# One level of Strassen's algorithm in the input projection of a hybrid attention layer, its weights prepared on the chip

## The chip, the cores and the metric

The kernel runs on one core of a Trainium2 chip. The metric is the device time of one execution in microseconds. Three runs of the kernel before took 1495.16, 1495.91 and 1497.05 us; the median is 1495.91 us. A second, profiled execution gives the trace that the text reads.

Five engines run their own instruction streams: PE (TensorE: matmuls and transposes), DVE (VectorE), ACT (ScalarE), POOL (GpSimd) and SP (SyncE), which in this kernel issues every DMA. Each works through its stream in the order in which the program wrote it, and waits on semaphores of the others. Matmul results land in PSUM banks, all other tiles in SBUF.

## What is computed

One layer on a sequence of 1024 tokens of width 1024, in float32. The input projection has 3080 columns: queries, keys and values of eight forgetting heads, eight gate columns, and queries, keys and values of eight chunked heads.

```python
h = rmsnorm(x, g_mix_pre[l])
proj = h @ w_in[l]                      # 1024 x 1024 by 1024 x 3080
y_fox = forgetting_attention(fq, fk, fv, f_logit)
y_chk = chunked_relpos_attention(cq, ck, cv, rel_bias[l])
y = concat(rmsnorm(y_fox), rmsnorm(y_chk))
x = x + rmsnorm(y @ w_out[l], g_mix_post[l])
x = x + rmsnorm(memory_cross_attention(rmsnorm(x, g_mem_pre[l]), mem_n, ...), g_mem_post[l])
x = x + rmsnorm(square(relu(rmsnorm(x, g_ff_pre[l]) @ w_ff1[l])) @ w_ff2[l], g_ff_post[l])
```

A forgetting head attends to all earlier tokens, with a bias from the cumulated log of its gate; a chunked head attends to its own chunk of 64 and the eight before it, with a bias by relative position.

## The kernel before

**Precision.** Every float32 operand of a product is split into a high part (rounded to the matmul's format) and a low part (the rest), and each product is three matmuls: high by high, high by low, low by high (`mm3`, L191 to L195). A split is a copy on ACT and a difference on DVE or POOL.

**Prologue** (L1346 to L1398, an order written out by hand). Rows of x are loaded, normalised (`norm_x`), turned by PE into the layout with features on partitions and split (`to_T`, L208 to L232). While this goes on, the values of four forgetting and four chunked heads are computed (`values`, in two groups of 256 columns; group 0 also has the eight gate columns) from weights that `value_weights` loads and `value_split` splits.

**Attention phase** (`attention_phase`). A planner (`Flow`) writes the order of all engines. It keeps a time for each engine, takes the next step of PE from the first of several streams that is ready, and places the work of the other engines with costs given in the code. The streams, by rank: products of probabilities and values (`value_steps`), transposes of probabilities (`turn_steps`), scores (`score_steps`), small jobs (`side_steps`), and as filler the rest of the projection (`filler_steps`: `project_steps` for query, key and late values of each pair of heads, 16 matmul groups for each block of 128 columns), then the memory's keys and values (`memory_steps`). `Stock` loads weights in order (tag `wraw`, three buffers) and splits them into the tags `whi` and `wlo` (two buffers each) or into the pool `u4`. Chunked heads 0 to 3 come first, then the forgetting heads, then the other chunked heads (`ORDER`). Scores are padded to at least 256 columns (`wide = max(w, 256)`, L581). Where a query block doesn't see a key block, `turn_steps` has POOL write zeros into that quarter (L665, L666), and `value_steps` multiplies all four quarters (L708, L709). Each block of outputs is summed from two halves by ACT (L715) and DVE (L716) and stored to DRAM (`od`). `forget_gates` computes the gates' bias from the projection's eight columns, in two exponentials and a logarithm on ACT and passes on DVE.

**After it.** `second_filler` begins with the output projection of the forgetting heads (`mix_steps(0)`), then of the chunked heads (`mix_steps(1)`), then memory attention and the MLP, which is already a Strassen product of one level. The MLP is not touched.

Of the kernel before, what the change touches and what calls it, by code (L numbers as in the profile page):

```python
# [14 lines left out]
F32 = mybir.dt.float32  # L15
# [7 lines left out]
P = 128  # L23
# [112 lines left out]
def build(ctx, tc, nc, out, t):  # L136
# [16 lines left out]
    def u4(name, shape, dt=F32R):  # L153

        return up.tile(list(shape), dt, tag="u4", bufs=30, name=name)
# [16 lines left out]
    wcount = [0]  # L172

    def load_w(src, shape, alloc=None, lo_on=None):
        n = wcount[0]
        wcount[0] += 1
        raw = wp.tile(shape, F32, tag="wraw", bufs=3, name=f"wraw{n}")
        nc.sync.dma_start(raw, src)
        return split_w(raw, shape, n, alloc, lo_on)

    def split_w(raw, shape, n, alloc=None, lo_on=None):
        if alloc is None:
            hi = wp.tile(shape, F32R, tag="whi", bufs=2, name=f"whi{n}")
            lo = wp.tile(shape, F32R, tag="wlo", bufs=2, name=f"wlo{n}")
        else:
            hi, lo = alloc(f"whi{n}", shape), alloc(f"wlo{n}", shape)
        nc.scalar.activation(hi, raw, AF.Copy)
        (lo_on or nc.gpsimd).tensor_sub(lo, raw, f(hi))
        return hi, lo

# [15 lines left out]
    def rms(x, scratch, name):  # L206
        ss = small.tile([P, 1], F32, tag="ss", bufs=8, name=f"ss_{name}")
        nc.scalar.activation(scratch, x, AF.Square, scale=1.0 / 32.0, accum_out=ss)  # L208
        return rstd_of(ss, f"rstd_{name}")

    def to_T(xa, xb, act, c0, name, tags=("tr", "tr")):

        trs = [mm_tile([P, 2, 2, P], f"tr_{name}_{k}", tags[k // 4]) for k in range(0, KC, 2)]

        def turn(k, q):
            xn = (xa, xb)[q]
            for j in range(2):
                nc.tensor.transpose(trs[k // 2][:, j, q, :], xn[:, (k + j) * P:(k + j + 1) * P], ident)

        ahead = tags[0] != tags[1]  # L220
        if ahead:
            for k in range(0, KC, 2):
                turn(k, 0)
        for k in range(0, KC, 2):
            if not ahead:
                turn(k, 0)
            turn(k, 1)
            src = trs[k // 2].rearrange("p a q b -> p a (q b)")
            i, o = k // act.per, k % act.per
            dh = act.h[i][:, o:o + 2, c0:c0 + 256]  # L230
            nc.scalar.activation(dh, src, AF.Copy)
            nc.vector.tensor_sub(act.l[i][:, o:o + 2, c0:c0 + 256], src, f(dh))  # L232


# [6 lines left out]
    ones = const.tile([1, P], F32, name="ones")  # L241
    nc.vector.memset(ones, 1.0)
# [3 lines left out]
    od = [[dr.tile([P, HT], F32, name=f"od{k}_{h}") for h in range(2)] for k in range(KC)]  # L246
# [3 lines left out]
    md = [dr.tile([P, D], F32, name=f"md{b}") for b in range(2)]  # L250
# [3 lines left out]
    p1s = ExitStack()  # L254
    p1 = pool("p1", stack=p1s)
# [6 lines left out]
    hT = [Act(f"hT{h}") for h in range(2)]  # L262
    def load_x(b):
        tag = "sp" if b % 3 else "klo"
        xt = p1.tile([P, D], F32, tag=tag, bufs=5 if b % 3 else 4, name=f"x_{b}")
        nc.sync.dma_start(xt, t["x"][b * P:(b + 1) * P, :])
        return xt

    def norm_x(xt, b):
        junk = p1.tile([P, D], BF16, tag="ph", bufs=2, name=f"junk{b}")  # L270
        r = rms(xt, junk, f"x{b}")
        nc.vector.scalar_tensor_tensor(xt, xt, r, gpre, op0=ALU.mult, op1=ALU.mult)
# [3 lines left out]
    def bias_rows(part):  # L276

        if part == 0:
            rows.extend(p1.tile([8, 768], F32, tag="sp", bufs=5, name=k) for k in ("rrow", "rsrc"))
# [8 lines left out]
    fcol = p1.tile([P, TB, 8], F32, tag="o2", bufs=2, name="fcol")  # L288

    def value_weights(g, raws=None, only=None):  # L290

        n = 264 if g == 0 else 256
        src = t["w_v0"] if g == 0 else t["w_v1"]
        raws = [] if raws is None else raws
        for i, (a, b) in enumerate(((0, 3), (3, 6), (6, 8)) if g == 0 else ((0, 4), (4, 8))):
            if only in (None, i):
                raw = wp.tile([P, b - a, n], F32, tag="wraw", bufs=3, name=f"wrawv{g}{a}")
                nc.sync.dma_start(raw, src[:, a:b, :])
                raws.append(raw)
        return raws  # L300

    def value_split(g, raw, i, lo_on=None):
        k = raw.shape[1]
        wh, wl = split_w(raw, list(raw.shape), f"v{g}{i}", None if g == 1 else u4, lo_on)
        return [(wh[:, j, :], wl[:, j, :]) for j in range(k)]

    def value_tiles(g):

        return [u4(f"vs{g}_{i}", (P, 2, 4, P)) for i in range(4)]

    def values(g, w, vs, kb):
        act, cs = hT[kb // 4], slice((kb % 4) * P, (kb % 4 + 1) * P)
        n = 264 if g == 0 else 256
        ps = mm_tile([P, n], f"v{g}_{kb}")
        for kc in range(KC):
            mm3(ps, act.hi(kc, cs), act.lo(kc, cs), *w[kc], kc == 0, kc == KC - 1)
        src = ps[:, 0:256].rearrange("p (h d) -> p h d", d=64)
        dh = vs[kb // 2][:, kb % 2, :, 0:64]
        nc.scalar.activation(dh, src, AF.Copy)
        if g == 0:  # L320
            nc.scalar.activation(fcol[:, kb, :], ps[:, 256:264], AF.Copy)
        nc.vector.tensor_sub(vs[kb // 2][:, kb % 2, :, 64:128], src, f(dh))


    ORDER = (("c", 0), ("c", 1), ("f", 0), ("f", 1), ("f", 2), ("f", 3), ("c", 2), ("c", 3))
# [3 lines left out]
            dict(s=2, tr=2, pv=2, mm=2, sp=1, p=2, klo=4, bias=2, raw=2, w=0, u4=6,  # L329
# [16 lines left out]
    class Stock:  # L346
# [3 lines left out]
        def __init__(self):  # L350
            self.blocks = []
            for n, (kind, pr) in enumerate(ORDER):
                if n == 5:
                    self.blocks.append("norm")
                b = (0 if kind == "f" else 8) + pr
                self.blocks.append((("q", n), t["w_qk"][b], [P, KC, P]))
                if n > 3:
                    self.blocks.append((("v", n), t["w_v"][n - 4], [P, KC, P]))
                if n == 7:
                    self.blocks.append("mem")  # L360
                self.blocks.append((("k", n), t["w_qk"][b + 4], [P, KC, P]))
# [53 lines left out]
        def split_now(self, n):  # L415
            for _ in range(n):
                key = self.to_split.pop(0)
                self.hi(key)
                for half in range(2):
                    self.lo(key, nc.gpsimd, half)  # L420
# [1642 lines left out]
```

## Time and profile before

| what | value |
|---|---|
| median of three runs | 1495.91 us |
| span of the profiled execution, first to last instruction | 1496.5 us |
| PE waits longest for another engine | 2.6 us in four places, products of probabilities and values |
| DMA traffic of the execution | 218.58 MB, 146 GB/s on average |
| DMA in the first 60 us | 8.00 MB |

The profile gives no other time of its own execution than the span; the span is 0.6 us above the median of the runs. In the rows, "L193" is line 193 of the kernel, "out<-in" names the tiles, and a row of the timeline gives start and duration in us, the engine, the line, the operation and, in brackets, how long the engine had been idle before it and what ended that. "PEld" is the loading of a matmul's stationary operand, which overlaps PE. A matmul's duration is the time until its end in the pipeline; what one costs in a row of them is the distance between their starts.

### The profile page before, as it was taken

Reading aid. Unit: us, or ns where it says so; the run is one execution under the profiler, and the core shown is the slowest. Engines: PE = TensorE matmul, PEld = TensorE weight load, DVE = VectorE, ACT = ScalarE, POOL = GpSimd, SP = SyncE. Lnnn points to the kernel's source line nnn. Section 1 sums busy time; section 2 is a strip of 40 time slices with the busy share of each in tenths; the row PEclk is TensorE's granted clock in tenths of the full one; section 3 lists DMA queues with packets and bytes.
Section 4 is the critical chain, followed back from the end, with each engine's and each line's share of the span. In section 5 each row is a group of like instructions: output and inputs, shape, how many; then the busy total and the mean of one; then the engine's idle time right before and its main releaser. Section 6 shows DMA issues by size and latency. Waiting matters only on the chain. (4 is left out here: it accounts for less than half of the span.)

```text
span 1496.5 us, 21618 instructions
## 1 busy us (share of the span) xinstructions
PE 1475.1 (99%) x7628; PEld 1254.1 (84%) x7628; DVE 938.1 (63%) x1617; ACT 789.8 (53%) x1405; POOL 403.4 (27%) x629
## 2 busy tenths in 40 slices
PE   8999999999999999999999999999999999999998
PEld 7989888888889888888888887888888888888886
DVE  6377677565576834884375577775555675646577
ACT  5367576575666835554354455555555553444442
POOL 4244355353354300521031423333333000000021
PEclk9999999999999999999999999999999999999999
DMA  4223312512225552461241355774445685436465
GB/s 170 90 74 89 84 44 88 152 55 65 73 66 149 173 177 85 137 213 59 85 169 57 112 183 186 265 246 147 150 150 176 234 340 202 140 120 215 173 252 197
DMA packets 82766, 218.58 MB, mean 146 GB/s; under 512 B 9801, under 2 KB 13905, under 8 KB 82658
## 3 DMA queue, kind: packets, MB, share of 16 engines
q1 hardware_dynamic: 82658, 217.20, 43.5%
q8 instruction: 60, 0.98, 0.3%
q14 instruction: 48, 0.39, 0.1%
HBM read 157.86 MB, written 50.91 MB: 140 GB/s over the span
## 5 line engine op out<-in xcount | busy, mean ns | idle before, releaser
L677 DVE TENSOR_TENSOR pl<-ptr,ph 128x512 fp32r<-128x512 f32 (+1 forms) x152 | 92.2, 616 | 39.7 <-ACT ph L680 33.7
L1789 ACT ACTIVATE whif<-ra 128x1024 fp32r<-128x1024 f32 x37 | 39.2, 1060 | 122.2 <-PE fy L194 62.6
L1791 DVE TENSOR_TENSOR wlof<-ra,whif 128x1024 fp32r<-128x1024 f32 x37 | 45.3, 1225 | 91.0 <-ACT whif L1789 91.0
L680 ACT ACTIVATE ph<-ptr 128x512 fp32r<-128x512 f32 (+1 forms) x152 | 79.3, 540 | 39.0 <-PE ptr L671 32.4
L1905 POOL TENSOR_SCALAR rf<-sf 128x1 f32<-128x1 f32 x8 | 8.2, 1026 | 326.4 <-ACT jf L1890 326.1
L709 PE MATMUL pv<-pl,vs 128*128 128x256 f32 x304 | 78.9, 283 | 2.6 <-DVE pl L677 2.6
L708 PE MATMUL pv<-ph,vs 128*128 128x256 f32 x304 | 79.8, 286 | 0.0
L194 PE MATMUL fx<-vlof,whif 128*128 128x512 f32 x168 | 65.4, 389 | 0.0
L193 PE MATMUL fx<-vhif,whif 128*128 128x512 f32 x168 | 65.4, 389 | 0.0
L195 PE MATMUL fx<-vhif,wlof 128*128 128x512 f32 x168 | 65.4, 389 | 0.0
L709 PEld LDWEIGHTS pv<-pl,vs 128*128 128x128 f32 x304 | 57.6, 189 | 7.4 <-DVE pl L677 2.2
L708 PEld LDWEIGHTS pv<-ph,vs 128*128 128x128 f32 x304 | 57.3, 188 | 4.0
L1679 POOL TENSOR_TENSOR sc<-wf,wf 128x512 f32<-128x512 f32 x14 | 21.3, 1524 | 142.3 <-DMA wf<-in_w_ff 95.4
L193 PE MATMUL k<-hT_hi,whik 128*128 128x512 f32 x128 | 52.7, 412 | 0.0
L193 PE MATMUL mq<-h2T_hi,whimq 128*128 128x512 f32 x128 | 51.6, 403 | 0.0
L193 PE MATMUL q<-hT_hi,whiq 128*128 128x512 f32 x128 | 50.9, 398 | 0.0
L193 PE MATMUL ym<-whimo,oT_hi 128*128 128x512 f32 x128 | 50.3, 394 | 0.1
L194 PE MATMUL yw<-wlowo,yT_hi 128*128 128x512 f32 x128 | 49.9, 390 | 0.3 <-DVE wlowo L410 0.3
L195 PE MATMUL k<-hT_hi,wlok 128*128 128x512 f32 x128 | 50.2, 392 | 0.0
L194 PE MATMUL mq<-h2T_lo,whimq 128*128 128x512 f32 x128 | 50.1, 391 | 0.1
L193 PE MATMUL yw<-whiwo,yT_hi 128*128 128x512 f32 x128 | 50.1, 392 | 0.0
L194 PE MATMUL k<-hT_lo,whik 128*128 128x512 f32 x128 | 50.1, 391 | 0.0
(596 smaller groups left out, 5029.2 us busy)
## 6 DMA issues: line engine op xcount, KB each, us to landing
ra<-gd SPq DMA_DIRECT2D x56, 512.0 KB, 3.9
wg<-in_w_ff SPq DMA_DIRECT2D x56, 512.0 KB, 6.0
wf<-in_w_ff SPq DMA_DIRECT2D x38, 512.0 KB, 4.0
gd<-s SPq DMA_DIRECT2D x48, 256.0 KB, 2.1
wrawmq<-in_w_mq SPq DMA_DIRECT2D x16, 512.0 KB, 3.8
wrawmo<-in_w_mo SPq DMA_DIRECT2D x16, 512.0 KB, 3.8
gd<-u SPq DMA_DIRECT2D x32, 256.0 KB, 2.1
gd<-g SPq DMA_DIRECT2D x25, 256.0 KB, 2.5
```

The costliest lines, as they stand in the source:

```text
L193: nc.tensor.matmul(ps, lh, rh, start=start, stop=False, skip_group_check=more)
L194: nc.tensor.matmul(ps, lh, rl, start=False, stop=False, skip_group_check=more)
L195: nc.tensor.matmul(ps, ll, rh, start=False, stop=stop, skip_group_check=more)
L677: flow.put("V", at, 0.7, lambda: nc.vector.tensor_sub(pl[:, live, :], tr[:, live, :], f(ph[:, live, :])), done)
L680: flow.put("S", flow.end, 0.6, lambda ph=ph, tr=tr, live=live: nc.scalar.activation(ph[:, live, :], tr[:, live, :], AF.Copy), split)
L708: nc.tensor.matmul(pv, v, ph[:, hs, :], start=c == 0 and half == 0, stop=False)
L709: nc.tensor.matmul(pv, v, pl[:, hs, :], start=False, stop=c + 1 == len(steps) and half == 1)
L1679: eng.tensor_sub(sc[:, k1], r0[:, k0], r1[:, k0])
L1789: nc.scalar.activation(ah, ra, AF.Copy)
L1791: nc.vector.tensor_sub(al, ra, f(ah))
L1905: nc.gpsimd.tensor_scalar(r, ssf[b][:, 0:1], ssf[b][:, 1:2], EPS, op0=ALU.add, op1=ALU.add)
```

## The change

With x split into quadrants by feature half and token half, and each pair of weight blocks (query and key columns of two heads, or 512 columns of forgetting values and 512 of chunked values) split into quadrants by feature half and column kind, one level of Strassen's algorithm (in Winograd's form) makes seven products of what were eight. Four sums of the weights and four sums of x's quadrants are formed first, and seven sums of the results afterwards.

- **x** comes a second time, transposed by the host (`x_t`). The rows are loaded only for their squares; the inverse norms are written to DRAM (`rsd`) and read back spread over all partitions (`rstd4`), and multiply the transposed tiles (`norm`). The first two value products use x times its gain alone and scale their rows afterwards.
- **Prologue.** Two value products; the first query product of all eight pairs from the two quadrants of the first 512 tokens (`q_prod`, with weights loaded and split in the loop), their finals, and a stored first product (`pqd`); meanwhile sums of x; memory rows are normalised and turned here; gate products (`gate_prod`); then the other five value products with their sums, with the gate chain cut into four pieces between them (`gate_chain`).
- **Attention phase.** Each pair has five products left (`pair_steps`); POOL forms the weight sums and copies the high parts (`pair_sums`, `pair_splits`), DVE the low parts. Queries, keys and values all go to DRAM (`qkd`, `vsd`) and are fetched for each head (`Heads`). Forgetting heads come first. After the pairs the filler is: memory keys, the output projection of the forgetting heads (results stored in `yd`, read back by `Back`), memory values.
- **Probabilities by values.** No zeros are written: a matmul covers only the quarters that hold something, so it may be 128 columns wide. Outputs are copied by one ACT instruction and stored as two halves (`od` doubles); the halves are added when they are read back.
- **Planner.** `u4` has 33 buffers in place of 30; some costs and token counts differ; all splits of later weights have their low part on DVE.

```diff
-        return up.tile(list(shape), dt, tag="u4", bufs=30, name=name)
+        return up.tile(list(shape), dt, tag="u4", bufs=33, name=name)
...
+    def rstd4(ss, th):
+        r = rall[:, th * 4:th * 4 + 4]
+        nc.gpsimd.tensor_scalar(r, ss, EPS, None, op0=ALU.add)
+        nc.gpsimd.tensor_tensor(r, r, mhalf[:, 0:4], op=ALU.pow)
+        nc.sync.dma_start(rsd[th * 4:th * 4 + 4, :].rearrange("b p -> p b"), r)
+        rt = pro.tile([P, HT], F32, tag="rt", bufs=2, name=f"rt{th}")
+        row = rsd[th * 4:th * 4 + 1, :]
+        nc.sync.dma_start(rt, bass.AP(tensor=row.tensor, offset=row.offset, ap=[[0, P], [1, HT]]))
+        return rt
...
-    ORDER = (("c", 0), ("c", 1), ("f", 0), ("f", 1), ("f", 2), ("f", 3), ("c", 2), ("c", 3))
+    ORDER = tuple((kind, pr) for kind in "fc" for pr in range(4))
...
-                for half in range(2):
+                full = 1 if dead == [0] else 0
+                todo = [(full, ph), (1 - full, ph), (1 - full, pl), (full, pl)]
+                for m, (half, x) in enumerate(todo):
...
+                    qs_ = [k for k in (2 * half, 2 * half + 1) if k not in dead]
+                    k0, k1 = qs_[0], qs_[-1] + 1
+                    q0 = slots[k0][1]
+                    nc.tensor.matmul(pv[:, q0:q0 + k1 - k0, :], v, x[:, k0:k1, :], start=c == 0 and m == 0,
+                                     stop=c + 1 == len(steps) and m == 3, skip_group_check=True)
...
+        yield from prod("6", 0, 0, quads["T2"], ([("pair", n, 0), ("p1", n)], True, 2))
...
+        yield from prod("5", 1, 0, quads["T1"], ([("pair", n, 1)], True, 2))
...
+        yield from prod("7", 2, 0, quads["T3"], ([("pair", n, 2), key("u2")], False, 2))
...
+        yield from prod("3", 0, 4, quads["B22"], ([key("p5")], False, 0))
...
+        yield from prod("4", 1, 4, quads["T4"], ([key("u3")], False, 0))
...
+        for _ in zip(load_xt(0, 0, True), load_v(0, 0, True)):
+            pass
+        list(load_xt(0, 1))
+        list(load_v(0, 1))
+        xrow = [load_row(b) for b in range(4)]
...
+        def vsplit(raw, name, eng, cut=False):
+            w = [wp.tile([P, 2, HT], F32R, tag=x, bufs=2, name=f"{x}v{name}") for x in ("whi", "wlo")]
+            for c in (slice(0, 1), slice(1, 2)) if cut else (slice(0, 2),):
+                yield nc.scalar.activation(w[0][:, c, :], raw[:, c, :], AF.Copy)
+                eng.tensor_sub(w[1][:, c, :], raw[:, c, :], f(w[0][:, c, :]))
+            yield w
...
+        for kp in range(4):
+            list(load_xt(1, kp))
+        xrow += [load_row(b) for b in range(4, 8)]
...
+        def values_out(k, kb, src):
+            st = u4(f"vst{k}{kb}", (P, 8, P))
+            v = src.rearrange("p (h d) -> p h d", d=64)
+            nc.scalar.activation(st[:, :, 0:64], v, AF.Copy)
+            nc.vector.tensor_sub(st[:, :, 64:128], v, f(st[:, :, 0:64]))
+            nc.sync.dma_start(vsd[k][:, :, kb, :], f(st).rearrange("p (n x) c -> p n (x c)", x=2))
...
+        def split_q(n):
...
+            nc.scalar.activation(w[0], raw, AF.Copy)
+            nc.gpsimd.tensor_sub(w[1], raw, f(w[0]))
...
+        for s in range(9):
+            if s < 8:
+                qb[s] = mm_tile([P, HT], f"q{s}", ("mm", "s")[s % 2])
+                q_prod(s, 0, B11)
+            if s:
+                q_prod(s - 1, 1, B21)
...
+            if s < 8:
+                q_first(s)
+            if s + 3 < 8:
+                load_q(s + 3)
+                split_q(s + 3)
+            if s:
+                q_final(s - 1)
+            for call in items[:3 if s < 2 else 2]:
+                call()
...
+        vprod(X, quads["T2"], w, True)
+        w = vw(4, "s3")
+        gate_chain(4)
...
+        for b in range(4):
+            nc.vector.tensor_add(u2[b], X[b], p1v[b])
+        vprod(X, quads["T3"], w, False)
+        w = vw(3, "a22")
+        gate_chain(4)
...
+        for b in range(4):
+            g = g_pro(f"u3v{b}")
+            nc.vector.tensor_add(f(g), X[b], p1v[b])
+            nc.vector.tensor_add(f(g), Z[b], f(g))
+            values_out(1, 4 + b, f(g))
+        vprod(X, quads["T4"], w, False)
```

More of the change, by code (lines that the diff above doesn't have):

```diff
@@ new lines, in build, with __init__, pump, load @@
+    p1r = {}
+    class Firsts:
+        def __init__(self):
+            self.left = list(range(8))
+        def pump(self):
+            while self.left and free["g"].ready():
+                n = self.left[0]
+                if n and not there(("u3", n - 1)):
+                    break
+                self.left.pop(0)
+                free["g"].take()
+                def load(n=n):
+                    p1r[n] = g_tile(f"p1r{n}")
+                    nc.sync.dma_start(f(p1r[n]), pqd[n])
+                flow.load(flow.now, load, mark(("p1", n)), 3.0)
```

978 lines of the change are left out of this document (596 added, 382 removed).

## The prediction

> **What bounds the kernel now.** I read the busy table of the page, then the busy time in three stretches cut at stage borders, then the waits.
>
> ```profile
> span 1496.5 us, 21618 instructions
> ...
> PE 1475.1 (99%) x7628; PEld 1254.1 (84%) x7628; DVE 938.1 (63%) x1617; ACT 789.8 (53%) x1405; POOL 403.4 (27%) x629
> ```
>
> ```profile
> 0.00:65.50 65.50, 59.33 (x452) 55.90 (x453) 32.08 (x49) 30.35 (x62) 22.56 (x29) 1.00 0.34 124
> 65.50:517.00 451.50, 448.01 (x2730) 394.68 (x2729) 305.14 (x837) 294.39 (x612) 198.82 (x417) 1.00 0.32 94
> 517.00:545.00 28.00, 27.71 (x124) 22.69 (x123) 17.79 (x25) 15.04 (x22) 3.35 (x2) 0.94 0.59 190
> ```
>
> The columns behind each stretch are its length, the busy time of PE, weight loads, DVE, ACT and POOL, the granted clock, the DMA share and GB/s. PE is the bound everywhere. Work taken off PE is therefore worth its full price, and every stretch in which PE has nothing to do is lost in full. The first stretch is the prologue, the second the attention phase, the third the memory values.
>
> **Prices on PE**, from starts of back-to-back instructions.
>
> ```profile
> 12.69 0.28 PE L193 MATMUL v<-whiv,hT_hi 128*128 128x256 f32 x1
> ...
> 17.95 0.29 PE L195 MATMUL v<-whiv,hT_lo 128*128 128x256 f32 x1
> ...
> 33.14 1.91 PE L218 MATMUL tr_x<-ident,x 128*128 128x128 f32 x16
> 34.80 0.36 PE L193 MATMUL v<-whiv,hT_hi 128*128 128x264 f32 x1
> ...
> 533.04 0.39 PE L194 MATMUL mv<-wlomv,mT_hi 128*128 128x512 f32 x1
> ...
> 542.34 0.39 PE L193 MATMUL yw<-whiwo,yT_hi 128*128 128x512 f32 x1
> ```
>
> From 12.69 to 17.95 there are 44 steps: 0.1195 each at 256 columns. From 533.04 to 542.34 there are 41: 0.2268 at 512. Sixteen transposes take 34.80 - 33.14 = 1.66, or 0.104 each.
>
> **Step 1, the projection.** Before: 2 groups x 8 blocks x 8 x 3 = 384 matmuls of 256 in the prologue and 20 blocks x 2 x 8 x 3 = 960 of 512 in the attention phase: 45.9 + 217.7 = 263.6. After: values 7 products x 48, queries and keys 8 pairs x 7 x 12, together 1008 of 512: 228.6. Saved 35.0. Of these, 480 (108.9) stay under attention; 336 + 192 = 528 stand in the prologue.
>
> **Step 2, transposes and gates.** The 48 transposes of x behind the first product and the 32 of the late values go: 80 x 0.104 = 8.3. The gates get products of their own, 8 + 8 + 16 matmuls of 512: +7.3. The sixteen memory transposes only move.
>
> **Step 3, the end of attention.**
>
> ```profile
> 515.40 0.39 PE L709 MATMUL pv<-pl,vs 128*128 128x256 f32 x1 [1.63 <-DVE pl L677]
> ...
> 517.41 0.63 PE L194 MATMUL mv<-wlomv,mT_hi 128*128 128x512 f32 x1
> ...
> 519.97 0.63 PE L194 MATMUL mv<-wlomv,mT_hi 128*128 128x512 f32 x1
> ```
>
> There the filler is used up: PE waits 2.6 in four places, then runs six steps in 2.56, 0.427 each, before it is fast again: some 8 x 0.2 = 1.6. The moved output projection (192 x 0.2268 = 43.5) and the memory values fill this: -4. The Trainium skill ("TensorE: Matmul & The Clock Gate", the part on the clock gate) puts the drop behind an idle window of about 3.4 us; here 1.63 and three shorter waits sufficed, so I use the row.
>
> **Step 4, narrow products of probabilities and values.**
>
> ```profile
> L709 PE MATMUL pv<-pl,vs 128*128 128x256 f32 x304 | 78.9, 283 | 2.6 <-DVE pl L677 2.6
> ...
> L666 POOL MEMSET pl<- 128x128 f32 x80 | 16.4, 206 | 0.0
> ```
>
> 80 zeroed quarters go, and with them 160 of the 608 matmuls shrink from 256 to 128 columns. No row shows one of that width in this format. The transposes bound the gain: 160 x (0.1195 - 0.104) = 2.5. A price of the 512-column kind would bound the loss: 160 x 0.107 = 17. I take 0, nearest the 256-column row, since the score products pad narrow pieces to 256, which speaks against any gain. The same page of the Trainium skill, section "Back-to-back issue gap", gives N/2.4 + 2.5 ns, 56 ns at 128 columns: by that, as an estimate, 10 us would be saved. Its section "LDWEIGHTS" gives about 107 ns per load of 128 columns, and the 0.104 agrees with that one.
>
> **Step 5, the attention phase.** The stretch from 65.5 to 542.3 holds 476.8; it becomes 476.8 - 108.9 - 3.3 + 43.5 - 4 = 404. Even if DVE and ACT kept all they did (305 + 18, 294 + 15), that is 80% and 77%, so PE stays the bound. SP issues about 128 stores of outputs, 112 loads of heads and 72 transfers of pairs at 0.41 (row below): 128 us, hidden. Range for this phase: 0 to +20.
>
> **Step 6, the prologue.** Here I expect the loss. Old idle: 65.5 - 45.9 - 48 x 0.104 = 14.6. The new prologue holds 528 + 32 matmuls and 16 transposes: 128.7. Its idle time E is what decides.
>
> ```profile
> 1.13 0.82 SPq L266 DMA_DIRECT2D x<-in_x  x2
> ```
>
> ```profile
> 4.82 1.06 ACT L208 ACTIVATE junk<-x 128x1024 bf16<-128x1024 f32 x1 [2.81 <-DMA x<-in_x]
> ```
>
> ```profile
> GB/s 0 128 382 333 229 423 418 415 424 411 385 401 279 0 0 11 0 0 0 0 0 0 0 0 11 0 0 0 5 0 0 0 0 0 31 185 355 311 199 0
> ```
>
> ```profile
> gcol<-in_g_heads SPq DMA_DIRECT2D x1, 4.0 KB, 4.6
> ```
>
> ```profile
> wrawmq<-in_w_mq SPq DMA_DIRECT2D x16, 512.0 KB, 3.8
> ```
>
> ```profile
> L187 ACT ACTIVATE whiv<-wrawv 128x1024 fp32r<-128x1024 f32 x2 | 2.1, 1058 | 1.4 <-DMA wrawv<-in_w_v 1.4
> ```
>
> ```profile
> L188 DVE TENSOR_TENSOR wlov<-wrawv,whiv 128x1024 fp32r<-128x1024 f32 x1 | 1.2, 1221 | 0.0
> ```
>
> ```profile
> 10.78 2.92 POOL L188 TENSOR_TENSOR wlov<-wrawv,whiv 128x1024 fp32r<-128x1024 f32 x1 [1.79 <-ACT whiv L187]
> ```
>
> ```profile
> L1107 ACT ACTIVATE yw<-yw,rs 128x512 f32<-128x512 f32 x16 | 11.0, 689 | 26.9 <-PE yw L195 26.8
> ```
>
> ```profile
> 30.46 0.38 ACT L319 ACTIVATE vs<-v 128x256 fp32r<-128x256 f32 x1 [0.34 <-PE v L195]
> ```
>
> ```profile
> 33.33 0.85 DVE L322 TENSOR_TENSOR vs<-v,vs 128x256 fp32r<-128x256 f32 x2
> ```
>
> The last two rows show that an engine keeps the order of the program: the copy was ready at 30.84, DVE took its partner at 33.33, behind a norm written ahead of it. The same holds for ACT, POOL and SP.
>
> (a) *First two products.* The first 0.5 MB of x landed 3.7 after its issue, and the stream runs at about 0.415 MB/us. Half tiles of x and weights land at 4.2 to 5.8; ACT and DVE split them, and the second matmul can start at 7.4, on a slow clock (1.6). The products take 2 x 10.9 and end at 30.8. Idle 9.0.
>
> (b) *The first query.* It needs the normalised quadrant, which needs the inverse norms spread along columns: written out and read back through SP, behind 10 MB of loads (x twice, values). These take 3.4 + 10/0.415 = 27.5; a small load behind such a stream took 4.6. With write and read, 33; only then are the query weights issued (SP is in order), landing at 36. ACT 1.06 and POOL 2.9 split them: PE restarts at 40. Idle 9.2.
>
> (c) *The query loop.* ACT reaches its first copy-out at about 60, behind two more weight splits, four quadrant splits and four value blocks in lockstep with DVE. In each of the first five rounds it then copies (0.69), waits for a load issued only behind that copy's store (0.41 + 0.41 + 3.8), splits (1.06), finishes a query (0.6) and splits two quadrants (2.1): 9.1, where PE needs 5.4. Memory rows and gate parts add 8. So 60 + 45.5 + 8 = 113.5; POOL and the last three products follow (2.9 + 8.2), less what the last round has behind its split (3): 121.6. Work is 48.8 in 81.6; idle 32.8, of which I take 30.
>
> (d) *Before the third values product.* Its accumulators are read by DVE behind a piece of the gate chain, and that piece on ACT stands behind a weight split whose buffer is free only when the product before ends.
>
> ```profile
> 73.35 1.06 ACT L483 ACTIVATE fe<-fl 8x1024 f32<-8x1024 f32 x1
> 74.43 1.28 ACT L485 ACT_TABLE_LOAD   x1
> 75.73 1.06 ACT L485 ACTIVATE fl<-fu 8x1024 f32<-8x1024 f32 x1
> ```
>
> ```profile
> 74.79 0.68 DVE L484 TENSOR_SCALAR fu<-fe 8x1024 f32<-8x1024 f32 x1
> 75.50 1.21 DVE L486 SCALAR_TENSOR_TENSOR fe<-fu,fe 8x1024 f32<-8x1024 f32 x1
> ```
>
> Split 1.06, Exp 1.06, DVE 0.68, table 1.28, Ln 1.06, DVE 1.21, sum 0.69: about 7.5.
>
> (e) *Before the fourth.* Split 1.06, table and Exp 2.34, three DVE passes of 1.2, sum 0.7: 7.7 for the first bank. The other three come 2.8 apart (two sums, a copy on ACT, a difference): 16.2, less the 2.0 of products that run meanwhile: 14.
>
> (f) *Slow clock* behind three more gaps, 1.6 each: 5.
>
> E = 9 + 9 + 30 + 7.5 + 14 + 5 = 74.5. With each part at its low end (6, 5, 10, 3, 8, 2) it is 34, at its high end (11, 13, 40, 10, 18, 9) 101.
>
> **The sum.** 1496.5 - 35.0 - 8.3 + 7.3 - 4.0 - 14.6 + E = 1441.9 + E = 1516.4. The median of the runs is 0.6 under the span; forecast **1516**. Break-even is E = 54.6.
>
> **Rivals.** *The loop at PE's pace*: if weights land before ACT asks for them, (c) falls from 30 to 3 and (f) to 4: 1488, faster. It decides from (c) under 10. For it speaks that PE holds three queries in advance; against it, the order on ACT and SP. *The prologue hidden as before*: the old one lost only 14.6; with (b) 6, (c) 3, (d) and (e) 1, (f) 2, E = 22: 1464. Against it stand the reuse of two weight buffers and the program order. *Narrow products at the 512 price*: 1533; the padding of the scores speaks for it. *Attention bound by DVE*: with the forgetting heads first and half the filler, PE idles some 10 of 404: 1526; the 80% of step 5 speak against it.
>
> **Chances.** Forecast 0.47 (1503 to 1529 alone), loop at PE's pace 0.16, all hidden 0.11, narrow products 0.13, DVE 0.13. A measurement here tells 0.2% (3 us) from no change. Faster 0.26, within 0.03 (cut from the edges of the first two), slower 0.71. The range 1476 to 1536 leaves out the hidden prologue and the far end of narrow products.
>
> **What would show it.** PE's share in the first 200 us: near 128.7 of work spread over about 203. ACT waiting on query weights five times by 4 to 5 us; PE waiting about 7 and 14 on DVE between values products; 128-column products 0.12 apart; no wait over 2 us in the attention phase. PE near 90% busy there in the first 200 us would make the forecast wrong.

## The result, and the profile after

The changed kernel takes 1644.8 us (median of 4 runs, 1643.2 to 1648.6), the kernel before 1495.9 (4 runs, 1495.2 to 1497.1): a ratio of 1.100, 95% interval 1.0985 to 1.1016. It is slower, as forecast, but by 149 us and not by 20. The span of the profiled execution is 1641.9 us.

The head of the page, the busy table and, in 40 slices of 41 us, PE's busy tenths and the granted clock:

```profile
span 1641.9 us, 21103 instructions
...
PE 1476.2 (90%) x7216; PEld 1234.7 (75%) x7216; DVE 998.0 (61%) x1614; ACT 782.4 (48%) x1383; POOL 483.7 (29%) x516
...
PE   6546773989889899999999999999999999999998
...
PEclk9678876999999999999999999999999999999999
```

PE has 412 instructions fewer and is busy just as long (1476.2 against 1475.1): what the products save, steps at a lower clock take back. All that is lost lies in the first 18 slices. Busy time by stage, cut where the prologue ends, where the memory values end, and at the span's end (columns: stretch, length, busy time of PE, weight loads, DVE, ACT, POOL, granted clock, DMA share, GB/s):

```profile
0.00:250.80 250.80, 158.84 (x577) 122.23 (x577) 113.44 (x117) 83.71 (x113) 78.01 (x46) 0.80 0.41 145
250.80:731.60 480.80, 418.93 (x2510) 365.99 (x2511) 314.19 (x808) 270.05 (x594) 232.12 (x290) 0.95 0.72 214
731.60:1641.90 910.30, 898.40 (x4131) 746.47 (x4129) 570.34 (x691) 428.63 (x677) 173.56 (x180) 1.00 0.52 180
```

The prediction had 203.2, 404 and about 910. The third stage is as forecast. The prologue is 47.6 us longer, the attention stage 76.8 us; that is the whole miss of the profiled run. The same view for the prologue's parts (two first value products, query loop, value tail; between the last two, for 3.9 us, PE is busy with the last gate product):

```profile
0.00:44.40 44.40, 24.84 (x97) 19.70 (x97) 9.89 (x15) 24.48 (x36) 11.40 (x14) 0.92 0.77 279
44.40:158.90 114.50, 66.31 (x224) 50.08 (x225) 60.54 (x61) 35.96 (x50) 36.25 (x19) 0.72 0.47 160
162.80:250.80 88.00, 63.79 (x241) 49.43 (x240) 40.04 (x40) 21.73 (x25) 28.35 (x14) 0.84 0.16 53
```

PE's work in the prologue is 128.7 us at full pace by the prediction's counts, so 250.8 - 158.8 = 92.0 us are idle and 158.8 - 128.7 = 30.1 us are slow pace, with the ends of the last steps before each wait in it. Idle by part: 19.6 before the loop, 48.2 in it, 24.2 behind it. In the attention stage 480.8 - 418.9 = 61.9 us are idle, and 418.9 - 404 = 15 are slow pace or dearer instructions.

PE's waits up to 250.8 (what it waited for: us in total, times, longest):

```profile
PE tr_mem L876 <- DVE mem L870: 21.6, 2, 20.0
PE q L174 <- ACT pq L1596: 18.2, 4, 7.8
PE q L174 <- ACT B_hi L1525: 11.8, 1, 11.8
PE vx L174 <- DVE u3v L1741: 11.1, 4, 8.0
...
PE vx L174 <- DVE u2v L1734: 6.1, 1, 6.1
```

What ACT and DVE waited for most around the loop, from 40 to 165 and from 0 to 165:

```profile
ACT whiq L1508 <- DMA wrawq<-in_w_qk: 32.4, 4, 11.4
```

```profile
DVE ql L1606 <- ACT qh L1604: 36.2, 6, 11.2
```

And PE from 283 to 510, in the forgetting heads; the first line's 23.9 ends at 282.8:

```profile
PE X L174 <- DVE u L806: 25.2, 2, 23.9
PE pv L653 <- ACT ph L625: 5.9, 2, 4.9
PE ptr L616 <- POOL spf5g L560: 4.4, 1, 4.4
PE ptr L616 <- POOL spf7g L560: 4.1, 1, 4.1
```

Behind the 23.9, DVE's first sum waits for the reload of a stored first product, which SP issues at 276.40, behind four value stores that wait for DVE; DVE made those values only behind its splits of the second pair:

```profile
276.40 0.49 SPq L744 DMA_DIRECT2D p1r<-pqd  x1
```

```profile
281.95 0.69 DVE L806 TENSOR_TENSOR u<-X,p1r 128x512 f32<-128x512 f32 x1 [7.54 <-DMA p1r<-pqd]
```

What lies behind the 4.9 is on ACT, and POOL stands at the same moment (the timeline; in brackets the idle time before and who ended it):

```profile
344.60 0.38 ACT L662 ACTIVATE ot<-pv 128x256 f32<-128x256 f32 x1 [6.87 <-DMA od_1l<-ot]
```

```profile
345.52 0.54 POOL L506 TENSOR_SCALAR_AFFINE_SELECT biasf<-biasf 128x128 f32<-128x128 f32 x2 [9.13 <-DMA biasf<-cd]
```

ACT wants to copy an output and stands for the buffer, whose earlier content is still on its way to DRAM; POOL stands for a decay row that is still on its way in. Both take their work in order, so the softmax work behind them stands too. The transfers of this stage, after (250 to 735) and before (65 to 545; packets, MB and share of 16 engines; KB and median us to landing):

```profile
q1 hardware_dynamic: 49175, 103.12, 71.7%
...
biasf<-cd SPq DMA_DIRECT2D x8, 512.0 KB, 7.7
...
od_1l<-ot SPq DMA_DIRECT2D x32, 64.0 KB, 2.7
od_0h<-ot SPq DMA_DIRECT2D x32, 64.0 KB, 4.4
```

```profile
q1 hardware_dynamic: 22428, 47.22, 33.3%
...
od<-ot SPq DMA_DIRECT2D x64, 64.0 KB, 1.9
biasf<-cd SPq DMA_DIRECT2D x8, 512.0 KB, 4.0
```

A 64 KB store takes 2.7 to 4.4 in place of 1.9 (the fastest and the slowest of its four groups are shown), and a decay load 7.7 in place of 4.0, while the stage moves more than twice the bytes.

The slow pace is in PE's timeline. Behind a wait of 4.56 in the query loop:

```profile
69.42 0.79 PE L174 MATMUL q<-B_hi,whiq 128*128 128x512 f32 x1 [4.56 <-ACT pq L1596]
...
74.28 0.59 PE L176 MATMUL q<-B_hi,wloq 128*128 128x512 f32 x1
74.70 0.40 PE L174 MATMUL q<-B_hi,whiq 128*128 128x512 f32 x1
74.94 0.40 PE L175 MATMUL q<-B_lo,whiq 128*128 128x512 f32 x1
```

From 69.42 to 74.70 twelve steps take 5.28 us, 0.44 each, then 0.24: this wait costs about 12 x 0.21 = 2.6 us on top of itself.

### The profile page after: what moved, and what is told of

Its sections match the earlier page's. It is cut to its first block, busy times and chain, and to the rows that moved or that the text cites. A ratio compares the mean times of both kernels' runs of the same rounds, so it can differ in the third digit from the quotient of the medians.

```text
span 1641.9 us, 21103 instructions
## 1 busy us (share of the span) xinstructions
PE 1476.2 (90%) x7216; PEld 1234.7 (75%) x7216; DVE 998.0 (61%) x1614; ACT 782.4 (48%) x1383; POOL 483.7 (29%) x516
## 5 line engine op out<-in xcount | busy, mean ns | idle before, releaser
L625 ACT ACTIVATE ph<-ptr 128x512 fp32r<-128x512 f32 (+1 forms) x152 | 78.1, 536 | 37.6 <-PE ptr L616 35.4
L653 PE MATMUL pv<-pl,vs 128*128 128x256 f32 (+1 forms) x304 | 66.5, 301 | 5.3 <-DVE pl L622 5.2
L653 PE MATMUL pv<-ph,vs 128*128 128x256 f32 (+1 forms) x304 | 58.9, 276 | 5.9 <-ACT ph L625 5.9
L653 PEld LDWEIGHTS pv<-ph,vs 128*128 128x128 f32 x304 | 53.2, 192 | 14.0 <-ACT ph L625 7.2
L174 PE MATMUL q<-B_hi,whiq 128*128 128x512 f32 x64 | 31.8, 497 | 31.9 <-ACT pq L1596 18.2
L653 PEld LDWEIGHTS pv<-pl,vs 128*128 128x128 f32 x304 | 46.7, 192 | 7.3 <-DVE pl L622 7.0
L176 PE MATMUL yw<-whiwo,yT_lo 128*128 128x512 f32 x128 | 50.5, 394 | 0.0
L176 PE MATMUL mq<-h2T_hi,wlomq 128*128 128x512 f32 x128 | 50.0, 390 | 0.0
L175 PE MATMUL ym<-wlomo,oT_hi 128*128 128x512 f32 x128 | 49.9, 390 | 0.0
```

Source lines behind the costliest of these rows:

```text
L174: nc.tensor.matmul(ps, lh, rh, start=start, stop=False, skip_group_check=more)
L175: nc.tensor.matmul(ps, lh, rl, start=False, stop=False, skip_group_check=more)
L176: nc.tensor.matmul(ps, ll, rh, start=False, stop=stop, skip_group_check=more)
L625: flow.put("S", flow.end, 0.56, lambda ph=ph, tr=tr, live=live: nc.scalar.activation(ph[:, live, :], tr[:, live, :], AF.Copy), split)
L653: nc.tensor.matmul(pv[:, q0:q0 + k1 - k0, :], v, x[:, k0:k1, :], start=c == 0 and m == 0, stop=c + 1 == len(steps) and m == 3, skip_group_ ...
```

## The experiments

Times are of single runs unless an interval is given, against 1644.8 of the changed kernel; the kernel before took 1493.9 to 1496.5 on the chips used. Differences under some 4 us are not read. Theory: engines that take their work in order (SP, ACT, DVE, POOL) starve PE at places that can be named, and each starved stretch slows PE's clock. Rivals: the number of bytes, the narrow products, the clock alone.

**Query weights loaded ahead.**

```diff
         split_q(0)
+        load_q(3)
...
-                load_q(s + 3)
                 split_q(s + 3)
+            if s + 6 < 8:
+                load_q(s + 6)
```

> The loads of query weights 3, 4 and 5 are issued right behind the splits of weights 0, 1 and 2, and those of 6 and 7 behind the splits of 3 and 4, so that no load stands behind a store of a first part on SP. If ACT's wait for these loads (32.4 us in 4 waits between 40 and 165) is what starves the query loop, the waits vanish, DVE no longer stands 36 us behind ACT at the low halves, the memory rows come earlier and the loop (44.4 to 158.9 us) shrinks by 25 to 45 us: 1600 to 1620 us. If the loop is held by DVE's own order or by the granted clock (0.57 to 0.82 there), the waits move to another releaser and the time stays within 8 us of 1644.8.

Measured: 1639.1. ACT's 32.4 us for loads shrink to 11.2 in one wait, but it now stands 20.0 us, up from 13.8, for PE to free the weights' buffers, and the loop is only 8.6 us shorter:

```profile
43.90:149.80 105.90, 63.66 (x225) 48.27 (x226) 61.47 (x60) 35.90 (x50) 38.03 (x19) 0.75 0.50 167
```

The 25 to 45 us expected of the theory did not come. The wait that the prediction named exists, but behind it stand others of nearly the same length.

**Memory rows one round later** (`if s in (2, 3)` becomes `(3, 4)`).

> The transposes of the memory rows stand one round later in TensorE's order (rounds 3 and 4 in place of 2 and 3). If TensorE's 21.6 us at them is a cost of their place, 12 to 20 us go: 1625 to 1633 us. If it only shows how late ACT and DVE run in these rounds, TensorE waits for the first parts or the query splits instead and the time moves by less than 6 us: 1639 to 1650 us.

Measured: 1645.6. PE waits 11.1 at the memory rows and 26.8 for the first parts (21.6 and 18.2 before). The place of the transposes is not the cost; they show how late DVE and ACT are.

**Turns behind the loop.**

```diff
-            for call in items[:3 if s < 2 else 2]:
-                call()
...
+        for call in items:
+            call()
+        load_vs(0)
...
         later = sum_vs(1, nc.vector)
```

> The sums and splits of the normalised rows into T1, T2, T3, B22 and T4, and the loads of the value weights that take their tiles, stand behind the query loop in place of inside its rounds. If DVE and ACT, which do this work in order between the first and the final parts of the queries, set the pace of the loop, the loop's stretch (114.5 us for 48.8 us of products) shrinks to 65 to 85 us, and the work comes back as idle time of TensorE behind the loop, 25 to 45 us of it: 1630 to 1665 us in all. If the loop is held by its loads and the granted clock, its stretch stays over 100 us and the time rises to 1670 or more.

Measured: 1652.2. The loop and the stretch behind it, up to the end of the gate product:

```profile
43.10:130.10 87.00, 62.66 (x224) 47.47 (x224) 27.66 (x35) 26.07 (x40) 26.77 (x15) 0.75 0.47 166
130.10:167.70 37.60, 8.30 (x18) 5.20 (x17) 36.19 (x28) 12.12 (x12) 13.15 (x5) 0.55 0.34 110
```

Without the sums and splits the loop is 27.5 us shorter, 2 us above the range expected; they come back as a stretch in which DVE is busy 36.2 of 37.6 us and PE 8.3. So this work costs about as much in either place and has little cover in both.

**Both at once**, weights ahead and turns behind.

> Query weights loaded ahead, and the sums and splits of the normalised rows behind the loop: both edits at once. With the second alone the loop took 87.0 us (43.1 to 130.1) for 48.8 us of products. If the loads then set its pace, it falls to 60 to 72 us and the time to 1625 to 1640 us; if the final parts' evictions or the memory rows do, it stays over 80 us.

Measured: 1657.6, and the loop takes 93.4 us, no less than the 87.0 with the second edit alone. The loads do not set its pace in this form either; PE waits there 14.8 for the memory rows, 10.4 for the first split quadrant and 7.3 for first parts, and pays the clock (62.9 busy for 48.8 of work).

**Filled gaps**: seven times in the loop

```diff
+            if s not in (0, 4):
+                fill = mm_tile([P, HT], f"fill{s}", "tr")
+                for i in range(10):
+                    x = B11.at(i % 4)[0]
+                    nc.tensor.matmul(fill, x[:, 0:P], x, start=True, stop=True)
             if s:
                 q_prod(s - 1, 1, B21)
```

> Seven times in the query loop ten products of 512 columns that nothing reads stand ahead of the second products of a query block: 70 x 0.227 = 15.9 us more work for TensorE at full clock. If the loop loses time to a granted clock that falls in TensorE's gaps (0.72 on average over the loop, 66.3 us busy for 48.8 us of work), the products behind the fills run faster and the loop's stretch changes by -8 to +4 us: 1636 to 1649 us. If the clock in the loop doesn't follow the gaps, the fills cost 10 to 16 us: 1655 to 1661 us.

Measured: 1656.5, inside the second range, though the loop grew by less than its fills:

```profile
44.10:164.50 120.40, 78.34 (x295) 60.48 (x296) 59.89 (x61) 35.97 (x50) 36.73 (x19) 0.77 0.45 155
```

Busy time grows by 12.0 where 15.9 were added, and the loop by 5.9, with a new wait of 8.2 that the fills bring with them (their bank is still read by the gates). The granted clock rises from 0.72 to 0.77, so the products behind the fills do run faster, but to buy the clock with idle products doesn't pay here. Some 5 us of the 11.7 arise outside the prologue and stay unexplained.

**Norms ahead**: the loads of the second half's input and of rows 4 to 7 move behind the first query weights' loads.

> The loads of the second half's transposed input and of rows 4 to 7 (4 MB) are issued behind the round trip of the first four inverse norms and the first three query weights. If that round trip stands behind those loads (DVE waited 19.0 us for it, TensorE 11.8 us), the first query product starts at 35 to 39 us in place of 44.4 and 5 to 9 us go: 1636 to 1640 us. If the round trip is slow by itself it still starts after 42.

Measured: 1647.5; the first query product starts at 49.8. DVE's wait for the norms falls from 19.0 to 8.8, but ACT, in order, now stands 17.6 us at the squares of rows 4 to 7, ahead of the first query split. With those squares moved behind the second split:

> As the run with the norms ahead, and the squares of rows 4 to 7 on ACT, which there stood 17.6 us for their rows ahead of the first query split, come behind the first normalised splits and the second query split. If only that order kept the first query product late, it starts at 33 to 38 us in place of 44.4 (49.8 in that run), and 5 to 9 us go against the changed kernel if the loop keeps the lead: 1636 to 1640 us. If the loop's later rounds then wait for the second inverse norms instead, the lead is given back: 1641 to 1649 us.

Measured: 1647.9. The first query product starts at 35.6, 8.8 us earlier, as expected, and the loop ends at 159.0, as before: the lead is given back at the first parts, for which PE now waits 26.7 us in place of 18.2.

**Sums ahead of the gates** (the four sums with X in front of `gate_chain(4)` and of the evictions, before the T3 and the T4 product).

> DVE takes the four sums with X that release the banks for the T3 and the T4 product ahead of the gate operations and of the value evictions. If TensorE's waits there (6.1 and 11.1 us) come from DVE's order, as the prediction has it, 10 to 17 us go: 1628 to 1635 us, and the wait at T4 is under 3 us. If the sums are held by the weight splits on ACT and GpSimd that follow, the waits turn to those and less than 5 us go.

Measured: 1636.8. Both waits on DVE are gone and the tail from the gate product to the first attention product takes 78.8 us in place of 88.0; 7.8 us come back as a wait for the first pair's splits on ACT. The mechanism is as predicted; of the 17.2 us of waits it is worth 8.0, under the range expected.

**The start of attention.** Three edits at one wait (23.9 us): the second pair's loads and splits behind the last value evictions; that with the first reload ahead of the third pair's loads; the second pair's loads ahead and its splits behind, with the reload ahead as in the second. The third:

```diff
         stock.pair_raws(1)
-        stock.pair_now(1)
         for b in range(4):
             nc.vector.tensor_add(u2[b], Z[b], u2[b])
             values_out(0, 4 + b, u2[b])
+        stock.pair_now(1)
...
+        p1r[0] = g_tile("p1r0")
+        nc.sync.dma_start(f(p1r[0]), pqd[0])
```

> The load, sums and splits of the second pair of key and query weights stand behind the last value evictions in place of ahead of them. If the wait of 23.9 us at the first small product of attention is the reload of the first parts standing on SP behind stores that wait for these splits, it shrinks to 4 to 8 us and 16 to 22 us go: 1623 to 1629 us. If the reload itself is slow under the transfers of this stretch, the wait stays over 15 us and less than 8 us go.

> As the run before it with the second pair behind the last value evictions, and the reload of the first part of query block 0 issued right behind those evictions, ahead of the third pair's loads, for which SP waited there from 262.5 to 274.8 us. If the order on SP is what makes TensorE wait at the first small product (22.2 us in that run), the wait falls to 5 to 10 us and 10 to 17 us go: 1627 to 1635 us. If the transfers themselves are slow, it stays over 15 us.

> The second pair's loads stay ahead of the last value evictions, its splits stand behind them, and the reload of the first part of query block 0 follows the evictions at once. By the two runs before, what holds the first sum of attention is DVE standing at the second pair's splits, whose load comes late in both. With its load early and its splits late the wait at the first small product is 6 to 12 us in place of 23.9 and 10 to 15 us go: 1630 to 1635 us. If it stays over 18 us, the reload itself is late.

Measured: 1643.5, 1644.6, 1635.1, with waits of 22.2, 19.7 and 9.7 us. In the first two it is another engine each time: SP at the third pair's loads (262.5 to 274.8), then DVE, as the timeline of the second shows:

```profile
273.92 1.23 DVE L404 TENSOR_TENSOR wlop<-wrawq,whip 128x1024 fp32r<-128x1024 f32 x1 [13.27 <-ACT whip L403]
...
276.80 0.68 DVE L806 TENSOR_TENSOR u<-X,p1r 128x512 f32<-128x512 f32 x1
```

The sum that PE needs (L806) stands behind the second pair's splits, which stand behind that pair's load. Only the third edit shortens both queues, and gives 9.7 us; 9.7 us of wait are left. My first reading (the reload behind stores on SP) was one of two queues.

**Full-width value products**, with zeros as before.

> The products of the probabilities with the values are 256 columns wide again with zeros in the dead quarter, as in the kernel before. If the narrow ones (median pitch 0.14 us against 0.12 of the wide ones) cost what their pitch shows, 0 to 5 us go; if they also disturb the order, 5 to 17 us. If the loss of the attention stretch is elsewhere, the time stays within 6 us of 1644.8, and GpSimd's zero fills may add 0 to 5.

Measured: 1645.7. The narrow products cost and save nothing that can be measured in the time. The pitch of 0.14 in this expectation is a misreading, set right under step 4.

**Transfers planned longer**: the order of work is laid out with `at + took * 1.8`.

> The order of work in the attention stretch is laid out with transfers 1.8 times as long as the program assumes (2.2 to 4.5 us; the trace shows 3 to 8 us to landing), nothing else differs. If the stretch loses its time because ACT, GpSimd and TensorE stand in order at work whose transfer lands later than planned, the waits of 4 to 9 us at output buffers, decay rows and memory rows shrink and 15 to 35 us go: 1610 to 1630 us. If the engines or the width of the transfers bind, the time moves by less than 8 us.

Measured: 1636.1. PE's two waits of 4.4 and 4.1 are gone, and POOL waits 7.4 us for decay rows in place of 22.9; ACT still waits for output buffers (17.5 us in 7, 13.1 in 4 before). The wait of 24 us at the start of the stage stays. The plan's short transfers are a part of the loss, and a smaller one than expected.

**Fewer bytes, more bytes.**

```diff
+            if a:
+                qs[n, a], kd[n, a], kl[n, a] = qs[n, 0], kd[n, 0], kl[n, 0]
+                mark(("head", n, a))(flow.now + 5.0)
+                return
```

> The second head of each pair takes the query and key tiles of the first head, so 48 of the 96 loads of 256 KB (12.6 of 103.7 MB in the attention stretch) are left out, and the second heads' scores are computed from the first heads' rows. If the transfers (71.7% of the DMA engines there, 5 to 8 us to landing against 2 to 4 before) make the stretch slow, it shrinks by 12 to 30 us: 1615 to 1633 us. If the order of the engines or their work binds, the time moves by less than 6 us.

```diff
+            flow.load(flow.now, lambda: nc.sync.dma_start(spare[a], t["w_v"][a, 0]))
```

> Each of the 16 head fetches also copies 512 KB from DRAM to DRAM, 8.4 MB more in the attention stretch and nothing that waits for it. If the transfers make the stretch slow, the time rises by 8 to 25 us: 1653 to 1670 us. If not, it rises by less than 4 us.

Measured: 1637.1 and 1677.5. The attention stage of the lighter and of the heavier kernel:

```profile
250.30:724.40 474.10, 420.72 (x2509) 368.53 (x2510) 312.62 (x806) 269.82 (x594) 224.56 (x289) 0.94 0.61 191
```

```profile
248.10:767.10 519.00, 433.26 (x2511) 378.47 (x2512) 314.70 (x808) 272.99 (x595) 226.34 (x290) 0.90 0.70 213
```

PE's work is the same in both; the lighter kernel leaves out the second heads' own queries and keys. With the copies, whose data nothing waits for, the stage is 38 us longer, through idle time (85.7 in place of 61.9) and through the clock (433.3 busy in place of 418.9). That is more than expected. The two loads of each head's keys land in 7.1 and 8.4 us in place of 5.5 and 6.8. But the planner counts each copy as 0.55 us of issue and lays the rest out anew: PE's order is that of the changed kernel for the first 710 of its 7216 instructions only, so the 38 us are bytes and another order together. Taking 12.6 MB away gives 6.7: from 283 to 510 PE is busy 11.4 us longer in the same time, but in the order laid out for the lighter load it later meets a wait of 8.9 on DVE. So both runs move as late transfers would have it; how much of the loss is theirs, this pair doesn't say.

**Attention light**: the second pair loaded first, longer transfers in the plan and half the head loads.

> The second pair loaded first, the longer transfers in the plan and half the head loads (as in that run, the second heads' scores come from the first heads' rows) at once, which leaves the prologue as it is. If late transfers are what is left of the attention stretch's loss, it falls from 480.8 us to 440 to 455 and the time to 1605 to 1620 us, since the waits at output buffers and decay rows go. If it stays over 460, the rest is the engines' order and the clock behind each small wait.

Measured: 1618.5, and the stage is 453.2 us long, both in the range expected for late transfers:

```profile
248.90:702.10 453.20, 415.46 (x2511) 365.93 (x2512) 314.71 (x807) 270.51 (x594) 226.88 (x290) 0.96 0.64 200
```

The single gains were 9.7 + 8.7 + 7.7 = 26.1, and together they give 26.3; 9.7 of that is the order at the start, so the hit in the range is no proof that late transfers are all of the loss. Some 49 us over 404 remain, 37.7 of them idle; the largest wait is 12.9 on DVE at a chunked head.

**Five orders at once**: norms ahead, weights ahead, sums ahead, second pair loaded first, longer transfers; then the same with the squares behind the splits.

> All order edits that gave time back: norms ahead, query weights ahead, sums ahead of the gate operations, the second pair loaded first and split last, and the attention laid out with longer transfers. If the losses lie one behind the other, the gains add up: 5.7 + 8.0 + 9.7 + 8.7 and what the norms give (5 to 9), 1603 to 1612 us. If each gain only uncovers the next engine in order, half of it is left: 1618 to 1628 us. It stays slower than the kernel before either way.

> The five order edits with the squares behind the splits, where the earlier run of five had them ahead. If the later start of the query loop there (48.5 us) cost what it shows, 8 to 14 us go against that run: 1593 to 1600 us. If the loop gives the lead back at its memory rows and first parts, it stays at 1602 to 1610 us.

Measured: 1607.0 (4 runs, 1604.5 to 1608.9; ratio to the kernel before 1.074, 1.0722 to 1.0758) and 1601.1 (4 runs, 1597.9 to 1606.2; ratio 1.0708, 1.0682 to 1.0735), the second between its two ranges. It has, by stage:

```profile
0.00:230.30 230.30, 155.01 (x576) 120.01 (x576) 116.94 (x117) 83.46 (x113) 80.69 (x46) 0.84 0.46 161
230.30:692.10 461.80, 422.57 (x2511) 369.84 (x2512) 315.51 (x808) 269.81 (x593) 230.52 (x290) 0.95 0.75 225
692.10:1598.40 906.30, 896.76 (x4130) 745.27 (x4128) 569.22 (x691) 429.66 (x678) 172.32 (x180) 1.00 0.52 179
```

The gains of edits at different places add up and more (43.8 against 29.0 for the sum of the single runs, the norms counted at -3.1); those at one place, in the query loop, don't. The best version found is still 7% slower than the kernel before.

## Why the prediction was right in direction and wrong in size

*Steps 1 and 2 (products saved):* right. The third stage is as forecast, and PE's busy time less its slow pace, 1476.2 - 45 = 1431, is within 8 us of the counts, 1475.1 - 36 = 1439.

*Step 3 (the end of attention, -4):* not borne out. PE's waits for the probabilities' low halves are 5.2 us in seven places in the stage, where they were 2.6 in four, and one of 5.0 for a memory load at 575 us comes with them.

*Step 4 (narrow products at 0):* right. The kernel orders four products as wide, narrow, narrow, wide, and a row of the timeline merges two of them:

```profile
330.52 0.35 PE L653 MATMUL pv<-ph,vs 128*128 128x256 f32 x2
330.71 0.44 PE L653 MATMUL pv<-pl,vs 128*128 128x128 f32 x2
330.99 0.40 PE L544 MATMUL sf1g<-kd,qs 128*128 128x512 f32 x1
```

The four take 0.47 here; the median is 0.461 over 66 such groups at full pace, and 0.476 over 57 groups of four wide ones. So a narrow product costs 0.11, near the sign "128-column products 0.12 apart", and the 160 save about 1 us; the 0.14 came from halving the second row, which holds a narrow and a wide step. The page "TensorE: Matmul & The Clock Gate" of the Trainium skill, section "Back-to-back issue gap", has 0.056 for a product by itself and about 0.081 in a stream with weight loads; the trace agrees with neither. The rival "at the 512 price" is out.

*Step 5 (attention stays PE bound, 404, range 0 to +20):* this is the step that failed, with 76.8 us. "SP issues ... 128 us, hidden" counted the issues and not the transfers: the landing times grew by half to more than double, and the order of work had been laid out for the short ones. The signal "no wait over 2 us" was wrong five times. Of the 76.8 us, 24.4 are the start of the stage, which the prediction did not look at: there the first sum waits for a reload that stands on SP behind value stores, and these wait for splits on DVE. The runs that shortened these queues (9.7), stretched the plan (8.7) and took bytes away (7.7) gave 26.3 together; the first two are shown as causes by their runs, while in the third fewer bytes and a new order of work are not told apart. The other 49 us, idle time in several waits and the clock behind them, are not taken apart, and their cause stays open. The rival "bound by DVE" finds no support: DVE is busy 314 of 481 us, and PE idles 61.9 and not 10.

*Step 6, (a) and (b):* 18.2 forecast, 1.6 of it slow clock; 19.6 idle measured, and 3.1 of slow pace. The reason for (b) was half right: the loads ahead delay the norms, but with them gone the first query waited for the squares, and with both gone the loop gave the lead back.

*Step 6 (c), the loop (30):* mis-sized; 48.2 idle. The prediction added what ACT does in each round, with its wait for weights as the cause. That wait was there, in four waits of 8 us in place of five of 4 to 5, and loading ahead shortened the loop by 8.6 us. What the sum left out is most of DVE's work: 60.5 us busy in the loop for 48.8 of products, and 36.2 us in which it stands behind ACT's copies. Without the sums and splits the loop was 27.5 us shorter; what makes up the rest of its idle time is not taken apart. The two faster rivals, the loop at PE's pace and the prologue hidden, are out by the 48.2.

*(d) and (e):* 7.5 and 14 forecast; 6.1 and 11.1 measured at these two waits, and moving the sums ahead took both away. The mechanism is shown.

*(f), the clock (5):* mis-sized by far; 30.1 in the prologue, and up to 15 in the attention stage. The sum had three more gaps at 1.6 each. The prologue has nine of over 4 us. Behind seven of them the pace is halved for 3.0 to 6.9 us, which costs 1.5 to 3.1; behind two, short waits follow so closely that it stays halved for 20 and 13 us, which costs half of PE's busy time there, 5.9 and 5.0:

```profile
44.36:64.45 20.09, 11.70 (x23) 7.20 (x24) 14.95 (x16) 6.63 (x9) 8.91 (x4) 0.50 0.29 69
218.55:231.70 13.15, 10.01 (x21) 6.54 (x22) 10.08 (x13) 2.52 (x4) 0.00 (x0) 0.50 0.45 159
```

The nine add up to 27 of the 30.1. So the price was right for the cheapest gaps, and their number and the chains of waits were missed.

E came to 92.0 + 30.1 = 122.1 in place of 74.5, above its high end of 101. So of the miss of 124 us, 18 are the loop's idle time, 25 the clock in the prologue, 77 the attention stage; the other 4 are spread over (a) to (e).

## What to carry to other kernels

A level of Strassen takes an eighth off the products and adds sums, splits and spills that must all find cover; in a stage where DVE has as much of this work as PE has products, price the glue first, by engine and in program order. When a change doubles the bytes of a stage, re-measure the landing times that its order of work assumes: copies that nothing waited for, and the order that was laid out around them, cost 33 us here. And price each gap of PE with the slow steps behind it, and ask how many gaps there will be.

## What the runs showed of the hardware

The store of the inverse norms is 2 KB in 512 pieces of four bytes. In the run with the norms ahead other loads were in flight for its first 2 us only, and SP, which waits for it before it issues the read, shows:

```profile
18.22 0.39 SPq L223 DMA_DIRECT2D rsd<-rall  x1
25.94 0.34 SPq L226 DMA_DIRECT2D rt<-rsd  x1
```

```profile
GB/s 412 431 412 417 358 110 3 0 0 0 0 0 0 0 0 66 110 215 363 445 393 403 435 403 431 417 412 440 403 431 431 393 417 234 52 19 0 0 0 0
```

It takes 7.7 us from its issue until SP goes on, with the channel empty for most of it (slices of 0.875 us from 15 to 50). The page "DMA: Bandwidth & Descriptors" of the Trainium skill, section "Anatomy of one DMA — SWDGE (gpsimd) path", puts the fixed part of a transfer that GpSimd issues at about 2 us. This one is issued by SP and is all small pieces, so it does not test that figure.

The clock: a wait of 1.33 us leaves PE's pace as it was, in two rows of the changed kernel:

```profile
299.62 0.50 PE L174 MATMUL X<-T_hi,whip 128*128 128x512 f32 x1 [1.33 <-DVE u L806]
299.96 0.39 PE L175 MATMUL X<-T_lo,whip 128*128 128x512 f32 x1
```

Behind waits of 4.1 to 5.0 it is halved for 3 to 6 us. The Trainium skill ("TensorE: Matmul & The Clock Gate", the part on the clock gate) has half rate behind an idle window of some 3.4 us and again full rate after one of work. These rows agree with it. Others do not, and the prediction's row with four short waits is not alone; two of them:

```profile
252.20:255.60 3.40, 3.40 (x9) 2.63 (x9) 1.49 (x2) 0.00 (x0) 0.00 (x0) 0.50 1.04 341
719.80:723.20 3.40, 3.40 (x10) 2.63 (x9) 3.23 (x4) 2.52 (x5) 0.70 (x1) 0.50 0.99 305
```

Here the granted clock is 0.50 behind waits of 1.76 and 0.53 us, and there behind one of 0.89; in the 3.4 us ahead of them, at full clock, PE was busy for 1.11 and 2.45 us. What decides in such stretches these runs do not show.
